# Rows of the last layer norm loaded into other buffers ahead of the accumulator rows, and three output tiles instead of two taking the bias by accumulating stores

## The chip, the cores and the metric

The kernel runs on one core of a Trainium2 chip. The metric is the device time of one execution in microseconds, here the median of three executions. One further execution was taken with the hardware profiler, and all rows below come from that one.

## What is computed

One layer of a post-norm decoder over 512 tokens of width 1024: a layer norm, a mixer with three branches, a residual layer norm, then a hierarchical mixture of experts and the last layer norm. The change lies in the last line of this part of the reference; `f` is the sum of the experts' outputs per token.

```python
x = layer_norm(ALPHA * x + m, ln1_g[l], ln1_b[l])
f = hierarchical_moe(x, w_rg[l], b_rg[l], w_re[l], b_re[l], w_up[l], w_down[l])
x = layer_norm(ALPHA * x + f, ln2_g[l], ln2_b[l])

def layer_norm(x, g, b):
    xf = x.astype(jnp.float32)
    mu = jnp.mean(xf, axis=-1, keepdims=True)
    var = jnp.mean(jnp.square(xf - mu), axis=-1, keepdims=True)
    y = (xf - mu) * lax.rsqrt(var + LN_EPS)
    return (y * g.astype(jnp.float32) + b.astype(jnp.float32)).astype(x.dtype)
```

## The kernel before

All arithmetic is fp32, with matrix products made of three passes over high and low parts. The experts' work is cut into 18 blocks of at most 128 tokens (`seq`, `nb` = 18), most of them one expert each. A block gathers its token rows, multiplies by the up weights, gates, and multiplies by the down weights (`down_mm`, L1211). The results of blocks 0 to 14 are copied from PSUM to a buffer named `yb` (`down_ev`, L1226; three buffers that take turns) and added to the rows of a DRAM accumulator `acc_d` by an indirect DMA of GpSimd with addition (`scatter`, L1232). The results of the last three blocks stay on chip (`down_split`, L1240) and are added by matrix products with 0/1 matrices `oht` that put each row at its token.

The end works on four tiles of 128 tokens. `acc_load(t)` (L1237) fetches tile t of the accumulator (512 KB) from DRAM by SyncE's queue. `combine(t, n)` (L1437) makes six matrix products for one half (512 columns) of a tile and adds them on VectorE to the accumulator row, with the row sum as a by-product. `ln2_var(t)` (L1447) makes the negative mean on VectorE and the sum of squares on ScalarE. `center(t)` (L1452) is two VectorE instructions, (x - mean) times `g2`. `rstd_ops` (L119) is a chain of tiny VectorE instructions for 1/sqrt(var): ten for several tiles at once, eight for one tile. `finish(t, r)` (L1456) scales by 1/sqrt(var) and stores: for tiles 0 and 1 ScalarE multiplies and GpSimd issues one store with addition onto `out`, which already holds the bias; for tiles 2 and 3 VectorE multiplies and adds `b2`, and SyncE issues plain stores of half a tile.

The bias was put into `out` long before, at L954 to L956, by one DMA of ScalarE's queue that repeats the row `ln2_b` over the first 256 rows. The rows `ln2_g` and `ln2_b` for the end, each repeated over 128 partitions (512 KB), are loaded at L1386 to L1395 into `raw3`, a buffer that held an expert's down weights before.

Order is fixed by hand (`manual_schedule`): each engine and each DMA queue runs its instructions in the order of the program, and waits on semaphores for the rest. A buffer that takes turns is written again only when its last user is done. On SyncE's queue the order is: the last weight loads (L750), the two norm rows (L1392), the four accumulator tiles (L1238), the four plain stores (L1463). `weave(chain, fill)` (L143) sets the instructions of `fill` evenly between those of `chain`. After the end stands a branch for extra blocks (L1485), which was not entered in the profiled execution; at its exit GpSimd's sequencer waits for its DMAs, and at the program's exit (L1582) all engines meet.

Of the kernel before, what the change touches and what calls it, by code (L numbers as in the profile page):

```python
# [9 lines left out]
F32 = mybir.dt.float32  # L10
# [7 lines left out]
P = 128  # L18
D = 1024
# [19 lines left out]
EPS2 = EPS / ALPHA ** 2  # L39
# [14 lines left out]
def trunk(ctx, tc, x, mem, rows, cols, wz, wkv, pac, pb8, pb2, wax, ws, wo, wr, br, we, out):  # L54
    nc = tc.nc
    pe, dve, act, pool, sp = nc.tensor, nc.vector, nc.scalar, nc.gpsimd, nc.sync
# [86 lines left out]
    def weave(chain, fill=()):  # L143
        done = 0
        for i, f in enumerate(chain):
            f()
            while done * len(chain) < (i + 1) * len(fill):
                fill[done]()
                done += 1
# [100 lines left out]
    with ExitStack() as st_a:  # L250
# [106 lines left out]
        rstd, ops = rstd_ops(mv)  # L357
# [561 lines left out]
    for i in range(2 * NT):  # L919
        j = i - 1  # L920
        ps = mmps()
        mm_pair(i, ps, 0)
        if i == 6:
            ohe = so2.tile([P, NT, P], F32, name="xr2")
        if i:
            r_tr(j)
        if 0 < i < 5:
            prep_hi(0, i - 1)
        mm_pair(i, ps, 1)
        if i:  # L930
            router(j)
        if i and i % 2 == 0:
            t = i // 2 - 1
            ln1_tile(t)
            weave(scale_ops(t, 512, (0, 512)))
            put_x1(sp, t)
        if 0 < i < 5:
            prep_lo(0, i - 1)
        if i == 5:
            ops, rest = route_ops(0, 2)  # L940
            weave(ops)
        mm_pair(i, ps, 2)
        if i == 5:
            rank_mm(0)
            rank_mm(1)
        if i == 6:
            weave(pos_ops(0, 2) + rest)
        if i == 7:
            ops, rest = route_ops(2, 3)
            weave(ops)  # L950
        mm_pair(i, ps, 3)
        for e, u in pending.get(i, ()):
            load_unit(e, u)
        if i == 1:  # L954
            r = ROWS.index("ln2_b")
            act.dma_start(out[:2 * P, :], rows[r:r + 1, :].to_broadcast([2 * P, D]))  # L956
        if i == 7:
            rank_mm(2)
        wo_add(i, ps)
        wo_stats(i)  # L960
        if i + 3 < 2 * NT:
            load_xr(i + 3)
    t = NT - 1
# [341 lines left out]
    for b in range(nb):  # L1305
        p_ = seq[b]
        nxt = seq[b + 1] if b + 1 < nb else p_
        pu = up_mm(b)
        if b == 0:
            sp.dma_start(seen_d, xgi[1][0:1, 0:4])  # L1310
            for e, u in ((2, 1), (3, 0), (3, 1), (4, 0), (4, 1)):
                load_unit(e, u)
            dn_hi(0, 0)
            dn_hi(0, 1)
            pw = map_mm(ohs_s, NS, 1, 3)
            gws = map_gw(pw, NS, "s")
            h = gate_h(pu, gws, NS - 1)
            hT = h_ev(h_tr(h))
            dn_lo(0, 0, dve, None)
            transp(1)  # L1320
            dn_lo(0, 1, dve, None)
            pdn[0] = down_mm(0, hT)
            scatter(down_ev(pdn[0]), *where(0)[::2])
        elif b > 1:
            hT = h_ev(pth)
        if b == 3:
            blk["ixx"] = map_ix(pix, NCOLX, "x")
            gather(5, *where(5)[::2])
            gather(6, *where(6)[::2])
            weave(vals_x)  # L1330
            pwx = map_mm(ohs_x, NCOLX, 1, 3)
        if b == 4:
            blk["gwx"] = map_gw(pwx, NCOLX, "x")
        ix, gw, c = where(b)
        new = [seq[b - 1]] if b and (b == 1 or seq[b - 2] != seq[b - 1]) else []
        if b == nb - 1:
            break

        def dn_prep():
            for p1 in new:  # L1340
                pl = pools[p_] if nxt != p_ else xp if pools[p_] is hlp else hlp
                for n in range(2):
                    if b > 1:
                        dn_hi(p1, n)
                        dn_lo(p1, n, dve, pl)
                if at[p1] + 3 < E:
                    load_unit(order[at[p1] + 3], 2)

        if b == nb - 2:
            scatter(down_ev(pdn[b - 2]), *where(b - 2)[::2])  # L1350
        dn_prep()
        tail = []
        if b == 1:
            load_unit(order[5], 0)
        if b and nxt != p_:
            for i in range(3):
                prep_hi(nxt, i)
        if 3 < b < nb - 2:
            yb = down_ev(pdn[b - 2])
        held = b > 1 and seq[b - 2] == seq[b - 1]  # L1360
        if b and nxt != p_:
            if not held:
                prep_hi(nxt, 3)
            if b == 1:
                ops = oe_b + order_tokens()
                weave(ops[:8], [lambda i=i, c=c_: prep_lo(nxt, i, None, c, c + 512) for i in range(2) for c_ in (0, 512)])
                weave(ops[8:18], [lambda c=c_: prep_lo(nxt, 2, None, c, c + 512) for c_ in (0, 512)])
                tail = ops[18:] + [lambda: prep_lo(nxt, 3)]
            else:
                ops = []  # L1370
                if b == 2:
                    ohs_x, ops, vals_x = map_ops(blk["px"], blk["ohx"], NCOLX, "x")
                weave(ops[:5] or [lambda: None] * 3, [lambda i=i: prep_lo(nxt, i) for i in range(3)])
                tail = ops[5:] if held else ops[5:] + [lambda: prep_lo(nxt, 3)]
        if b and nxt != p_:
            for i in (2 * at[p_] + 9, 2 * at[p_] + 10):
                if i < 2 * E:
                    load_unit(order[i // 2], i % 2)
        if b:
            h = gate_h(pu, gw, c)  # L1380
        if 0 < b < nb - 1:
            transp(b + 1)
        weave(tail)
        if b + 4 < nb and b not in (1, 2):
            gather(b + 4, *where(b + 4)[::2])
        if b == nb - 2:  # L1386
            gb2 = mlate.tile([P, 2048], F32, name="raw3")
            g2, b2 = gb2[:, :D], gb2[:, D:]

            def load_gb(eng, i):  # L1390
                r = ROWS.index("ln2_g") + i
                eng.dma_start((g2, b2)[i], rows[r:r + 1, :].to_broadcast([P, D]))  # L1392

            load_gb(sp, 0)
            load_gb(sp, 1)  # L1395
        if 3 < b < nb - 2:
            scatter(yb, *where(b - 2)[::2])
        if b == nb - 4:
            oht = mox.tile([P, 4, T], F32R, name="rawx", bufs=2)
            row_hot(oht[:, 0], *where(nb - 3)[::2])  # L1400
        if b == nb - 3:
            for i in range(1, 3):
                row_hot(oht[:, i], *where(nb - 3 + i)[::2])
        if b > 1:
            pdn[b - 1] = down_mm(b - 1, hT)
            if b == nb - 2:
                ys.append(down_split(pdn[b - 1]))
            elif b < 3:
                scatter(down_ev(pdn[b - 1]), *where(b - 1)[::2])
        if b:  # L1410
            pth = h_tr(h)
        if held:
            prep_half(nxt, 3)
        if b == 2:
            pix = map_mm(ohs_x, NCOLX, 0, 1)
# [21 lines left out]
    def combine(t, n):  # L1437
        ns = halves_[n]
        ps = (mmps if n and t else auxps)()
        for i in range(3):  # L1440
            for k in range(2):
                pe.matmul(ps, lhsT=oht[:, i, t * P:(t + 1) * P], rhs=ys[i][:, k, ns],  # L1442
                          start=i + k == 0, stop=i + k == 3)
        dve.scalar_tensor_tensor(xs_[t][:, ns], ps, 1.0, xs_[t][:, ns], op0=ALU.mult, op1=ALU.add,
                                 accum_out=sums[:, t, n:n + 1])
# [8 lines left out]
                                                       op0=ALU.add, op1=ALU.mult) for ns in halves_]  # L1454

    def finish(t, r):  # L1456
        if t < 2:
            act.mul(zs[t], zs[t], r)
            pool.dma_start(out[t * P:(t + 1) * P, :], zs[t], accum_op=ALU.add)
        else:  # L1460
            for ns in halves_:
                dve.scalar_tensor_tensor(zs[t][:, ns], zs[t][:, ns], r, b2[:, ns], op0=ALU.mult, op1=ALU.add)
                sp.dma_start(out[t * P:(t + 1) * P, ns], zs[t][:, ns])  # L1463
# [4 lines left out]
        combine(t, 1)  # L1468
        ln2_var(t)
    weave(center(0))  # L1470
    r01, ops = rstd_ops(None, 2, sums[:, 0:2, 3], EPS2)
    weave(ops, [lambda: combine(2, 0), lambda: combine(2, 1), lambda: ln2_var(2)] + center(1))
    finish(0, r01[:, 0:1])
    finish(1, r01[:, 1:2])
    combine(3, 0)
    combine(3, 1)
    ln2_var(3)
    weave(center(2) + center(3))
    r23, ops = rstd_ops(None, 2, sums[:, 2:4, 3], EPS2)
    weave(ops)  # L1480
    finish(2, r23[:, 0:1])
    finish(3, r23[:, 1:2])

    n_extra = nc.values_load(blk["eix"][0:1, NEXTRA:], min_val=0, max_val=E - 1)
    with tc.If(n_extra > 0):  # L1485
# [100 lines left out]
```

## Time and profile before

| | us |
|---|---|
| Median of three executions (lowest, highest) | 917.89 (917.84, 918.22) |
| The profiled execution, its own time | 920.99 |
| Its span, first to last instruction | 919.2 |
| TensorE busy in it | 883.4 (96%) |
| VectorE busy | 588.8 (64%) |
| ScalarE busy | 460.6 (50%) |
| GpSimd busy | 58.1 (6%) |

Moments are given in us from the start of the span. The profiled execution took 3.1 us longer than the median of the others. The busy share is a mean over the whole span; the change touches only the last 60 us of it and one store near 643 us.

### The profile page before, as it was taken

How to read it: one execution, taken by the hardware profiler on the slowest of the kernel's cores; microseconds unless marked ns; L12 is line 12 of the kernel's file. 1: busy time of each engine (PE TensorE's matmuls, PEld its weight loads, DVE VectorE, ACT ScalarE, POOL GpSimd, SP SyncE). 2: the span in 40 equal slices, each digit the busy share in tenths (PEclk: the TensorE clock that was granted, in tenths of full speed). 3: DMA queues.
4: the chain of work that ended last, by engine and by line, in shares of the span. 5: the costliest groups of instructions: out<-in, count | busy, mean ns of one | idle time of the engine just before them, and what ended most of it. 6: DMA issues, size and time to landing. Idle time of an engine off the chain costs nothing.

```text
span 919.2 us, 11177 instructions
## 1 busy us (share of the span) xinstructions
PE 883.4 (96%) x4272; PEld 733.8 (80%) x4272; DVE 588.8 (64%) x1020; ACT 460.6 (50%) x656; POOL 58.1 (6%) x59
## 2 busy tenths in 40 slices
PE   9999999999999999999999999999998889999991
PEld 5778888889998888888878888788887678888870
DVE  6765773344555543345866865766768887689976
ACT  5545432223444342214678687534204657688942
POOL 0000100000000000000000000000001123233210
PEclk9999999999999999999999999999997989999996
DMA  8313632333322412221313322237673988899544
GB/s 339 123 46 115 218 126 97 112 112 109 121 93 92 142 46 91 102 79 73 129 62 106 138 73 88 92 109 279 229 286 112 409 320 274 269 285 405 146 151 96
DMA packets 29281, 144.70 MB, mean 157 GB/s; under 512 B 5461, under 2 KB 5717, under 8 KB 16166
## 3 DMA queue, kind: packets, MB, share of 16 engines
q1 hardware_dynamic: 21462, 127.25, 37.6%
q0 software_dynamic: 6048, 13.45, 5.8%
q10 hardware_dynamic: 1712, 3.24, 1.1%
q8 instruction: 35, 0.57, 0.3%
q14 instruction: 24, 0.20, 0.1%
HBM read 136.24 MB, written 17.30 MB: 167 GB/s over the span
## 4 chain that ended last, share of the span: by engine, by line
PE 78%; DVE 11%; ACT 5%; DMA 3%; issue 2%; SPq 0%; DVEq 0%; ACTq 0%
PE mm L109 61%; PE mm L1220 4%; PE aux L109 4%; PE mm L308 3%; DVE hl L767 2%; PE aux L1162 1%; DMA x<-in_x_dram 1%; DMA col<-in_cols_dram 1%; ACT hl L82 1%; PE aux L1442 1%; DMA o<-in_we_dram 1%; DVE hl L83 1%; PE aux L464 1%; DVE xs L83 1%; ACT hl L1200 1%
## 5 line engine op out<-in xcount | busy, mean ns | idle before, releaser
L109 PE MATMUL mm<-hl 128*128 128x512 f32 x1416 | 327.6, 390 | 0.2 <-DVE hl L83 0.2
L109 PEld LDWEIGHTS mm<-hl 128*128 128x128 f32 x1416 | 264.7, 188 | 54.6 <-DVE hl L83 0.6
L83 DVE TENSOR_TENSOR hl<-raw,hl 128x1024 fp32r<-128x1024 f32 (+1 forms) x116 | 136.3, 1181 | 136.7 <-ACT hl L82 136.2
L82 ACT CAST hl<-raw 128x1024 fp32r<-128x1024 f32 (+1 forms) x116 | 116.3, 1015 | 126.3 <-PE mm L109 113.8
L109 PE MATMUL mm<-o,hl 128*128 128x512 f32 x624 | 142.9, 389 | 1.2 <-ACT o L82 1.2
L109 PEld LDWEIGHTS mm<-o,hl 128*128 128x128 f32 x624 | 117.1, 188 | 25.8 <-ACT o L82 1.6
L109 PE MATMUL mm<-hl,xs 128*128 128x512 f32 x408 | 99.7, 401 | 0.0
L109 PEld LDWEIGHTS mm<-hl,xs 128*128 128x128 f32 x408 | 77.1, 193 | 15.9
L767 DVE TENSOR_TENSOR hl<-o,hl 128x1024 fp32r<-128x1024 f32 (+1 forms) x45 | 50.3, 1147 | 4.8 <-ACT hl L761 4.7
L1220 PE MATMUL mm<-hl,hT 128*128 128x512 f32 x196 | 49.5, 399 | 0.0
L761 ACT CAST hl<-o 128x1024 fp32r<-128x1024 f32 x42 | 41.9, 1051 | 4.2 <-PE mm L1220 4.2
L1220 PEld LDWEIGHTS mm<-hl,hT 128*128 128x128 f32 x196 | 35.6, 188 | 6.8
L1086 POOL DMA_INDIRECT y<-x_d,ixg x3 | 3.2, 1070 | 594.5 <-DVE rtl L1145 593.9
L224 ACT ACTIVATE gate<-mm,col 128x512 f32<-128x512 f32 x24 | 16.5, 688 | 39.7 <-PE mm L109 39.6
L1209 DVE TENSOR_TENSOR hl<-raw,hl 128x1024 fp32r<-128x1024 f32 x26 | 30.6, 1220 | 3.2 <-PE mm L109 1.6
L1200 ACT CAST hl<-raw 128x1024 fp32r<-128x1024 f32 x32 | 31.9, 1053 | 0.0
L109 PE MATMUL mm<-memT,hl 128*128 128x256 f32 x192 | 27.3, 286 | 0.2 <-ACT memT L82 0.2
L308 PE MATMUL mm<-o,hl 128*128 128x512 f32 x96 | 25.8, 421 | 0.9 <-ACT hl L82 0.6
L109 PEld LDWEIGHTS mm<-memT,hl 128*128 128x128 f32 x192 | 24.9, 191 | 0.9 <-ACT memT L82 0.4
L808 ACT COPY x1T<-aux 128x512 f32<-128x512 f32 x8 | 4.7, 587 | 40.6 <-PE aux L807 25.9
L109 PE MATMUL mm<-hl,yh 128*128 128x512 f32 x96 | 24.4, 400 | 0.0
L109 PE MATMUL mm<-hl,memT 128*128 128x256 f32 x192 | 24.3, 283 | 0.0
(337 smaller groups left out, 1157.8 us busy)
## 6 DMA issues: line engine op xcount, KB each, us to landing
raw<-in_wz_dram SPq DMA_DIRECT2D x30, 1024.0 KB, 4.7
o<-in_we_dram SPq DMA_DIRECT2D x21, 1024.0 KB, 8.0
raw<-in_we_dram SPq DMA_DIRECT2D x18, 1024.0 KB, 7.5
rawx<-in_we_dram SPq DMA_DIRECT2D x9, 1024.0 KB, 7.8
raw<-in_pac_dram SPq DMA_DIRECT2D x8, 1024.0 KB, 4.7
raw<-in_wkv_dram SPq DMA_DIRECT2D x8, 1024.0 KB, 4.7
raw<-in_pb_dram SPq DMA_DIRECT2D x4, 1024.0 KB, 6.2
raw<-in_wo_dram SPq DMA_DIRECT2D x4, 1024.0 KB, 4.9
```

The source lines that it names most:

```text
L82: act.copy(hi, src)
L83: dve.tensor_tensor(lo, src, hi.bitcast(F32), op=ALU.subtract)
L109: pe.matmul(ps, lhsT=a(sa_), rhs=b(sb_), start=first and i == 0, stop=last and i == 2)
L224: act.activation(store[j], ps, AF.Sigmoid, bias=cc(C_M + br_i * 8 + j))
L308: pe.matmul(ps, lhsT=xT(k, slice(t * P, (t + 1) * P))(sx), rhs=wv[2 * n + k // 4, k // 2 % 2][:, sw, k % 2, :], start=i == 0, stop=i == 23)
L464: pe.matmul(pv[:, ch * P:(ch + 1) * P], lhsT=v[:, ch, g * P:(g + 1) * P], rhs=wst[:, g, :], start=True, stop=True)
L761: act.copy(t[:, 0], raws[key, i // 2][:, (i % 2) * 1024:(i % 2 + 1) * 1024])
L767: (eng or dve).tensor_tensor(t[:, 1, c0:c1], src[:, c0:c1], t[:, 0, c0:c1].bitcast(F32), op=ALU.subtract)
L1162: pe.transpose(ps[:, j * P:(j + 1) * P], xg[:, k * P:(k + 1) * P], ident)
L1200: act.copy(dnh[key][:, :, n * 512:(n + 1) * 512], dn_half(key, n))
L1209: eng.tensor_tensor(dnl[key][n], dn_half(key, n), dnh[key][:, :, ns].bitcast(F32), op=ALU.subtract)
L1220: pe.matmul(ps, lhsT=hT[:, sa_, f, :], rhs=dn[sb_][:, f, :], start=i + f == 0, stop=i + f == 3)
```

## The change

The diff in full. The initial bias store covers three tiles instead of two. The two norm rows go into two `yb` buffers instead of `raw3`; on SyncE's queue they keep their place ahead of the accumulator tiles. Tile 2 is finished as tiles 0 and 1 are. The chain for 1/sqrt(var) is made once for tiles 0 to 2 and once for tile 3 alone, and `center`, `combine` and `ln2_var` are ordered anew around it.

```diff
         if i == 1:
             r = ROWS.index("ln2_b")
-            act.dma_start(out[:2 * P, :], rows[r:r + 1, :].to_broadcast([2 * P, D]))
+            act.dma_start(out[:3 * P, :], rows[r:r + 1, :].to_broadcast([3 * P, D]))
...
         if b == nb - 2:
-            gb2 = mlate.tile([P, 2048], F32, name="raw3")
-            g2, b2 = gb2[:, :D], gb2[:, D:]
+            g2, b2 = (mo.tile([P, D], F32, name="yb", bufs=3) for _ in range(2))
...
     def finish(t, r):
-        if t < 2:
+        if t < 3:
             act.mul(zs[t], zs[t], r)
             pool.dma_start(out[t * P:(t + 1) * P, :], zs[t], accum_op=ALU.add)
         else:
...
         combine(t, 1)
         ln2_var(t)
     weave(center(0))
-    r01, ops = rstd_ops(None, 2, sums[:, 0:2, 3], EPS2)
-    weave(ops, [lambda: combine(2, 0), lambda: combine(2, 1), lambda: ln2_var(2)] + center(1))
-    finish(0, r01[:, 0:1])
-    finish(1, r01[:, 1:2])
-    combine(3, 0)
-    combine(3, 1)
+    combine(2, 0)
+    combine(2, 1)
+    ln2_var(2)
+    weave(center(1))
+    r012, ops = rstd_ops(None, 3, sums[:, 0:3, 3], EPS2)
+    weave(center(2))
+    weave(ops, [lambda: None, lambda: combine(3, 0), lambda: None, lambda: combine(3, 1)])
+    finish(0, r012[:, 0:1])
     ln2_var(3)
-    weave(center(2) + center(3))
-    r23, ops = rstd_ops(None, 2, sums[:, 2:4, 3], EPS2)
+    finish(1, r012[:, 1:2])
+    finish(2, r012[:, 2:3])
+    weave(center(3))
+    r3, ops = rstd_ops(None, 1, sums[:, 3:4, 3], EPS2)
     weave(ops)
-    finish(2, r23[:, 0:1])
-    finish(3, r23[:, 1:2])
+    finish(3, r3[:, 0:1])
```

## Rows read from the trace of the kernel before

**Rows 1.** Waits of 880 to 920 us: waiter, releaser, total us, times, longest.
```profile
DVE y L1444 <- DMA y<-acc_d: 3.8, 1, 3.8
```
**Rows 2.** SyncE queue's own waits, 800 to 920 us, same columns.
```profile
SPq L1392 <- DVE o L1209: 24.7, 1, 24.7
```
**Rows 3.** Timeline of the end: start us, us, engine, line, operation, operands, count.
```profile
886.42 0.81 SPq L1392 DMA_DIRECT2D raw<-in_rows_dram  x2
887.40 2.17 SPq L1238 DMA_DIRECT2D y<-acc_d  x4
888.33 4.24 PE L1442 MATMUL aux<-hl,rawx 128*128 128x512 f32 x18
889.15 0.69 DVE L83 TENSOR_TENSOR hl<-mm,hl 128x512 fp32r<-128x512 f32 x1 [0.67 <-ACT hl L82]
893.60 0.69 DVE L1444 SCALAR_TENSOR_TENSOR y<-aux,y 128x512 f32<-128x512 f32 x1 [3.76 <-DMA y<-acc_d]
895.13 1.52 PE L1442 MATMUL mm<-hl,rawx 128*128 128x512 f32 x6
896.54 1.41 DVE L1453 SCALAR_TENSOR_TENSOR o<-y,ln2s,raw 128x512 f32<-128x512 f32 x2
897.99 0.17 DVE L125 TENSOR_SCALAR lnv<-ln2s 128x2 f32<-128x2 f32 x1
901.83 0.15 DVE L135 SCALAR_TENSOR_TENSOR lnr<-lnt,lnr 128x2 f32<-128x2 f32 x1
902.02 2.19 ACT L1458 ACTIVATE o<-o,lnr 128x1024 f32<-128x1024 f32 x2 [0.64 <-DVE lnr L135]
903.46 1.91 POOL L1459 DMA_DIRECT2D out_dram<-o  x2 [26.71 <-DVE ln2s L1449]
904.11 1.13 ACT L1450 ACTIVATE yb<-y,ln2s 128x1024 f32<-128x1024 f32 x1
906.02 0.16 DVE L125 TENSOR_SCALAR lnv<-ln2s 128x2 f32<-128x2 f32 x1
907.99 2.74 DVE L1462 SCALAR_TENSOR_TENSOR o<-o,lnr,raw 128x512 f32<-128x512 f32 x4
908.76 2.51 SPq L1463 DMA_DIRECT2D out_dram<-o  x4
```
**Rows 4.** GpSimd's accumulating stores of the end, L1459: issue to landing.
```profile
DMA to landing us min/median/max: 5.8/7.5/9.2
```
**Rows 5.** Last scatters, L1233, 858 to 877 us: duration min/median/max ns, starts; landing.
```profile
L1233 POOL DMA_INDIRECT acc_d<-yb,ix_x x3: 1545/1597/4546, 858.5 to 872.2; - x3
...
DMA to landing us min/median/max: 6.1/6.2/8.9
```
**Rows 6.** GpSimd's sequencer at the exit, L1485, then L1582: ns, starts.
```profile
L1485 POOLq EVENT_SEMAPHORE  x1: 7858/7858/7858, 905.9 to 905.9; - x1
L1485 POOLq INC_SWDGE_SEM  x1: 1031/1031/1031, 913.8 to 913.8; - x1
...
L1582 POOLq DRAIN  x1: 3498/3498/3498, 914.9 to 914.9; - x1
```
**Rows 7.** SyncE's sequencer at the exit, L1582: ns, first and last start.
```profile
L1582 SPq DRAIN  x2: 7/10/13, 917.5 to 917.6; - x2
```
**Rows 8.** SyncE's plain stores of the end, L1463: issue to landing.
```profile
DMA to landing us min/median/max: 5.5/5.6/5.6
```
**Rows 9.** Accumulator loads, L1238: issue to landing.
```profile
DMA to landing us min/median/max: 6.1/7.3/8.1
```
**Rows 10.** DMA packets, 904 to 914 us: queue, packets, MB, share of 16 engines.
```profile
q0 software_dynamic: 288, 1.05, 67.9%
q1 hardware_dynamic: 492, 0.91, 23.9%
```
**Rows 11.** DMA packets, 906.5 to 908 us, same columns.
```profile
q0 software_dynamic: 72, 0.29, 101.1%
```
**Rows 12.** The bias store near 643 us, L956: issue to landing.
```profile
DMA to landing us min/median/max: 9.9/9.9/9.9
```

## The prediction

> **What bounds the kernel now.** TensorE is busy 96% of the span, but the change lies behind its last matrix product, so I read the end in this order: the waits, the timeline, the landings of the stores, and last what each engine does at the exit. The first view shows one wait worth having: VectorE stands still for 3.76 us until the first accumulator tile arrives [rows 1, 3]. The products for it began at 888.33 and run 18 in 4.24 us, so the first six end near 889.7; VectorE was free at 889.84, and it starts only at 893.60. Why the tile is late is seen in SyncE's own waits: the load of the norm rows waits 24.7 us, till the split of the last down weights frees `raw3` [rows 2]. It goes out at 886.42, and the accumulator tiles stand behind it at 887.40; the first lands 6.1 us later [rows 3, 9].
>
> From 893.60 VectorE has no gap worth the name until 910.73, when the last half tile is done; its plain store goes out at about 910.8 and lands 5.5 us later, at 916.3 [rows 3, 8]. That looks like the end, and the chain of waits also ends on VectorE and SyncE. But SyncE is through with its exit work at 917.6 [rows 7], while the span ends at 919.2. The one who is later is GpSimd's sequencer: it waits 7.86 us from 905.9 for its accumulating stores, which is until 913.76, then spends 1.03 us on a semaphore instruction and 3.50 us in a drain, to 918.4 [rows 6]. This fits the landing of the second accumulating store, issued at about 904.5 and landed 9.2 us later [rows 3, 4]. So the end is set by the last accumulating store plus 919.2 - 913.76 = 5.44 us, and SyncE's path has some 0.8 us to spare. What the change does to that store decides.
>
> **The change, part by part.** *Norm rows into `yb`.* The two `yb` buffers belonged to the scatters issued at 858.5 and 865.3, landed some 6.1 and 6.2 us later, about 864.6 and 871.5 [rows 5]. SyncE's queue then has nothing else, so the rows load there and leave the way free. `acc_load` next waits for the last scatter, 872.2 + 8.9 = 881.1. Issued then with 6.1 us to the first landing, tile 0 is there by 887.3, before its products at 889.7: the 3.76 us of waiting go. The row loads share DMA engines with the two last scatters, so these may land up to about 1.4 us later each (512 KB at 380 GB/s, an estimate from 0.91 MB in 23.9% of 10 us [rows 10]); even with 2.4 us more the tile is in time. The junk buffer moves to the last scatter's `yb`, free at 881.1 and first needed after 891: nothing.
>
> What is late next is TensorE: with the data there, VectorE follows the products, six per 1.4 us, and gains nothing until the sixth half tile, whose products end at 895.13 + 1.52 = 896.65 [rows 3]. Center of tile 0 and the rest fit between.
>
> *New order on VectorE.* From 896.7: combine 0.7, mean 0.2, centers of tiles 1 and 2 at 1.41 each [rows 3] give 900.4. The ten small steps then have a pitch of 0.2 us (906.02 to 907.99 is ten of them without fill [rows 3]) and two combines of about 0.65 between them: 3.0 to 3.3 us, so 1/sqrt(var) for tiles 0 to 2 is there at about 903.4. Before, tiles 0 and 1 had it at 901.98 [rows 3]. So although 3.76 us of waiting are gone, the first ScalarE multiply starts 1.4 us later than before, since a third tile's statistics and center now lie ahead of it. For VectorE as a whole the end comes sooner: the two instructions that finished tile 2 are gone (1.37), the second chain has eight steps for ten (0.4). Center of tile 3 from 903.6 to 905.0; its chain waits for ScalarE's squares (below, 905.8) and takes 1.6; two last instructions end at 908.9 instead of 910.73.
>
> *ScalarE.* In order: multiply 0, squares of tile 3, multiply 1, multiply 2. A multiply has a pitch of about 1.05 (2.19 for two), the squares 1.04 and a read of 0.19 behind [rows 3]. From 903.45 the multiplies end at 904.6, 906.8 and 907.9.
>
> *GpSimd.* Its store starts 0.29 us after the multiply's end (903.17 to 903.46) and occupies it about 0.94 [rows 3]. So three stores start at 904.9, 907.1 and 908.1, against two at 903.46 and 904.5.
>
> *The accumulating store of tile 2.* This is the dear part. Beside no plain store, 72 packets took 101.1% of all sixteen DMA engines for 1.5 us and moved 0.29 MB [rows 11]: 194 GB/s, so 512 KB is 2.70 us of all engines. Plain packets need 23.9% of 10 us for 0.91 MB [rows 10]: 0.69 us for 256 KB, half as much per byte. The whole of the two accumulating stores with their slow start was 6.79 us, plain work beside it 2.39: 9.2 us, which is the time from the first store's issue done (904.40) to the second's landing (913.7). After the change: 6.79 + 2.70 + two plain stores of 0.69 each, 1.38, all of which now fall into this stretch = 10.9 us, counted from 905.8. Last landing 916.8; with 5.44 behind it the span ends at 922.3, 3.1 us later. The unknown is how evenly the sixteen engines share: lower bound with no plain store in the way 915.4, span 920.9; upper bound with a late engine as the second store had it (9.2 against 2 x 2.70 + about 2 of start), 1.9 more, span 924.2.
>
> *Bias store of three tiles.* One DMA either way, 1.5 instead of 1.0 MB, landed 9.9 us after issue near 643 [rows 12]. Half as much again lands at most 5 us later, and nobody touches `out` before 903. The loads beside it are for steps further on (`load_xr(i + 3)`, L962, three half tiles ahead), and TensorE works on meanwhile. I take nothing; if that cover were gone, at most those 5 us.
>
> A rule of the Trainium skill, "DMA: Bandwidth & Descriptors" (section on the anatomy of one DMA on GpSimd's path), speaks against my price: a DMA there costs about 2.0 us plus its bytes at 436 GB/s. For 512 KB that would be an estimated 3.2 us, so the third store would land near 911.3 and the span would end near 916.7. The trace does not agree: these stores took 5.8 and 9.2 us [rows 4], and while they had the engines to themselves they moved 194 GB/s [rows 11].
>
> **The rivals.** *The third store costs no time of its own.* If the stores overlap freely, the last lands as the first did alone, 5.8 us after its start: 908.1 + 5.8 = 913.9, where the last one lands now. The span is 919.3 and the time 918.0, no change. Faster still, down to the rate of plain packets: then SyncE's plain stores decide. The last goes out at 908.9, lands at 914.4, and 1.3 + 0.8 us of exit make 916.5, a time of 915.2. It decides from an accumulating landing before 911.1. The rule above of the Trainium skill, "DMA: Bandwidth & Descriptors", would lead close to this case. For it: early in the stretch the engines move little. Against it: a full DMA share right after.
>
> *The drain is no fixed cost behind the last store.* The 3.50 us of drain could wait for something else, which will be over. Then the end is 916.8 + 1.03 + 0.1 + 0.8 = 918.7, a time of 917.4, no change. For it: the drains of SyncE take 10 ns [rows 7]. Against it: GpSimd's begins right behind its own semaphore instruction, and nothing else in the rows ends at 918.4.
>
> *The change doesn't bring the accumulator tiles early* (the last scatter later than 885, or SyncE held up). Then VectorE starts near 893.6 as now, center of tile 0 ends at 897.95, and the chain is there at about 905.4 instead of 903.4: 2.0 us on top, a time of 923.0. The gaps that TensorE's pace would leave take up the rest.
>
> **How the numbers follow.** The profiled execution's span is 919.2 and its own time 920.99, 3.1 above the median 917.89; I take differences of the span and set them on the median. Forecast: 917.89 + 3.1 = 921.0, chance 0.62, own range 919.7 to 922.9. Third store for nothing: 0.07 no change, 0.11 faster. Drain not fixed: 0.15, no change. Tiles not early: 0.05. A measurement of this kernel tells some 0.2% (1.8 us) from no change. Slower 0.67, same 0.22, faster 0.11. The range 917.3 to 923.3 takes in forecast, the drain, the late tiles and the free store without gain; what is left out is the faster case and the ends.
>
> **What would show it.** Right: the wait of 3.8 us on `y<-acc_d` is gone, norm rows go out near 865 and 872, accumulator tiles near 881 to 883; first multiply of ScalarE near 903.4; stores of GpSimd near 904.9, 907.1, 908.1; its long semaphore wait ends near 917, about 5.4 us ahead of the end, and SyncE is ready some 5 us before. Wrong: a last accumulating landing before 914 (its price per byte was mistaken), or an end less than 3 us behind it (the drain was).

## The result, and the profile after

The changed kernel takes 923.91 us (median of four executions, 923.11 to 924.94) against 918.06 in the same session, a ratio of 1.0058 (95% interval 1.0045 to 1.0070); a second measurement of both on another occasion gave 924.22 and 1.0066 (1.0052 to 1.0079). It is slower, as forecast, and by more: the forecast was 921.0, 3.1 us above the kernel before, with 923.3 as upper end; the medians of the session differ by 5.85 us.

The waits of the end, 880 to 920 us, and SyncE's own from 800 us (waiter, releaser, total us, times, longest) answer to [rows 1, 2]:

```profile
DVE y L1443 <- DMA y<-acc_d: 1.8, 1, 1.8
...
SPq L1391 <- DMA acc_d<-yb,ix_x: 19.0, 2, 10.8
...
SPq L1238 <- DMA acc_d<-yb,ix_x: 6.4, 1, 6.4
```

VectorE's wait for the first accumulator tile has fallen from 3.8 to 1.8 us. SyncE no longer waits for a split of weights; it waits for the scatters. The timeline of the end, with the lines that answer to [rows 3] (line numbers are one lower there and in some kernels below):

```profile
886.70 1.75 SPq L1238 DMA_DIRECT2D y<-acc_d  x4
886.72 4.24 PE L1441 MATMUL aux<-hl,rawx 128*128 128x512 f32 x18
890.07 0.69 DVE L1443 SCALAR_TENSOR_TENSOR y<-aux,y 128x512 f32<-128x512 f32 x1 [1.84 <-DMA y<-acc_d]
901.61 1.15 ACT L1457 ACTIVATE o<-o,lnr 128x1024 f32<-128x1024 f32 x1 [4.19 <-DVE lnr L135]
903.06 0.94 POOL L1458 DMA_DIRECT2D out_dram<-o  x1 [20.90 <-ACT o L1457]
903.80 2.17 ACT L1457 ACTIVATE o<-o,lnr 128x1024 f32<-128x1024 f32 x2
905.23 0.87 POOL L1458 DMA_DIRECT2D out_dram<-o  x1 [1.23 <-DVE lnt L129]
905.59 1.41 DVE L1461 SCALAR_TENSOR_TENSOR o<-o,lnr,yb 128x512 f32<-128x512 f32 x2
906.26 0.84 POOL L1458 DMA_DIRECT2D out_dram<-o  x1 [0.17 <-issue]
906.37 1.00 SPq L1462 DMA_DIRECT2D out_dram<-o  x2
```

VectorE is done at 907.0 and the last plain store is out at 907.4, yet the span ends at 921.4. What lies between is the landing of GpSimd's stores and GpSimd's exit (landing after issue in us; then its sequencer's lines, duration in ns and start, as in [rows 4, 6]; then SyncE's as in [rows 7]):

```profile
DMA to landing us min/median/max: 5.7/6.8/9.2
...
L1487 POOLq EVENT_SEMAPHORE  x2: 43/4031/8019, 907.4 to 915.8; - x2
L1487 POOLq INC_SWDGE_SEM  x1: 1042/1042/1042, 915.9 to 915.9; - x1
...
L1584 POOLq DRAIN  x1: 3580/3580/3580, 917.0 to 917.0; - x1
...
L1584 SPq DRAIN  x2: 7/10/13, 917.7 to 917.7; - x2
```

The third store, issued at 906.26, lands 9.2 us later, near 915.4; GpSimd waits for it from 907.4 for 8.02 us, then spends 1.04 and 3.58 us, to 920.6. SyncE has been ready since 917.7, 3.7 us ahead of the end instead of the some 5 that were forecast.

The start of an execution moves by one to two us from one to the next whatever the kernel, so the kernels are compared below from the first product of the first combine (the line of TensorE at 886.72 above) to the end of the span, "the end" for short: 921.4 - 886.7 = 34.7 us here, 919.2 - 888.3 = 30.9 in the kernel before [rows 3].

### The profile page after: what moved, and what is told of

It reads as the page before. It is cut to its first block, busy times and chain, and to the rows that moved or that the text cites. A ratio compares the mean times of both kernels' runs of the same rounds, so it can differ in the third digit from the quotient of the medians.

```text
span 921.4 us, 11177 instructions
## 1 busy us (share of the span) xinstructions
PE 883.0 (96%) x4272; PEld 732.8 (80%) x4272; DVE 587.4 (64%) x1016; ACT 462.4 (50%) x657; POOL 68.0 (7%) x60
## 4 chain that ended last, share of the span: by engine, by line
PE 77%; DVE 12%; ACT 5%; DMA 2%; issue 2%; SPq 0%; ACTq 0%; POOLq 0%; POOL 0%; DVEq 0%
PE mm L109 61%; PE mm L1220 4%; PE aux L109 4%; PE mm L308 3%; DVE hl L767 2%; PE aux L1162 1%; DMA x<-in_x_dram 1%; DMA col<-in_cols_dram 1%; ACT hl L82 1%; DVE hl L83 1%; PE aux L464 1%; ACT hl L1200 1%; ACT hl L761 1%; DVE th L684 0%; PE aux L564 0%
## 5 line engine op out<-in xcount | busy, mean ns | idle before, releaser
L1220 PEld LDWEIGHTS mm<-hl,hT 128*128 128x128 f32 x196 | 36.4, 193 | 6.9
L1200 ACT CAST hl<-raw 128x1024 fp32r<-128x1024 f32 x32 | 31.9, 1053 | 0.0
L1233 POOL DMA_INDIRECT acc_d<-yb,ix_x x10 | 27.0, 2703 | 54.3 <-ACT hl L761 20.5
```

What stands on the lines that cost most here:

```text
L1200: act.copy(dnh[key][:, :, n * 512:(n + 1) * 512], dn_half(key, n))
L1220: pe.matmul(ps, lhsT=hT[:, sa_, f, :], rhs=dn[sb_][:, f, :], start=i + f == 0, stop=i + f == 3)
L1233: pool.indirect_dma_start(out=acc_d[:, :], in_=yb, in_offset=None, out_offset=bass.IndirectOffsetOnAxis(ap=ix[:, b:b + 1], axis=0), bounds ...
```

## The experiments

Nine kernels beside the two were run, and the two themselves again. Two of the nine leave something out: the one with plain GpSimd stores the bias of tiles 0 to 2, the one without the third store the result of tile 2. The table gives the measured ratio to the kernel before of the same session, and three distances from the first combining product, read from each profile: the issue of the first accumulating store, GpSimd's semaphore instruction that follows the last landing, and the end of the span.

| Kernel | Ratio (95%) | First store | Semaphore | End |
|---|---|---|---|---|
| before, on record | 1 | 15.1 | 25.5 | 30.9 |
| before, second profile | 1.0004 (0.9993, 1.0014) | 14.9 | 24.0 | 29.4 |
| before, third profile | 1.0004 (0.9994, 1.0014) | 15.3 | 24.6 | 30.0 |
| bias store of three tiles only | 0.9997 (0.9987, 1.0008) | 14.8 | 25.4 | 30.8 |
| norm rows moved only | 0.9984 (0.9975, 0.9993) | 13.4 | 22.8 | 28.2 |
| changed, early chain | 1.0021 (1.0012, 1.0030) | 13.4 | 25.8 | 31.3 |
| changed, tile 2 plain | 1.0036 (1.0023, 1.0049) | 16.3 | 26.4 | 32.3 |
| changed, no third store | 1.0031 (1.0019, 1.0043) | 16.3 | 26.0 | 31.9 |
| changed, plain GpSimd stores | 1.0015 (1.0005, 1.0025) | 16.3 | 25.0 | 30.5 |
| changed | 1.0058 (1.0045, 1.0070) | 16.3 | 29.2 | 34.7 |
| changed, again | 1.0066 (1.0052, 1.0079) | 16.3 | 29.6 | 35.0 |
| changed, rows late | 1.0083 (1.0070, 1.0096) | 18.2 | 30.9 | 36.4 |
| rows moved, all tiles plain | 0.9996 (0.9986, 1.0005) | none | none | 28.8 |
| rows moved, one accumulating store | 0.9975 (0.9965, 0.9986) | 13.4 | 20.0 | 27.7 |

**The kernel before, again.** No edit.

> The kernel before, unchanged, for a second profile of it. The one on record ran 3.1 us above the median, so the difference of the two profiles (2.2 us) falls short of the difference of the medians (5.9). Theory 1 (the end decides: the last accumulating landing plus a fixed exit): from the first product of the first combine to the end of the span it is 30.9 us again (888.3 to 919.2), and a span near 916.3 means that the stretch before it was some 3 us shorter in this execution. Theory 2 (the body differs between the kernels): the end is the same, but the stretches before it are steady and shorter than the changed kernel's.

Its profile has a span of 916.1 and starts the combining products at 886.71; the end is 29.4 us, not 30.9. GpSimd's semaphore instruction of this execution:

```profile
L1485 POOLq INC_SWDGE_SEM  x1: 1031/1031/1031, 910.7 to 910.7; - x1
```

So neither theory holds whole. 1.6 us of the difference between the two profiles of this kernel lie ahead of the end (888.33 against 886.71), and 1.5 us lie in the end itself. A body that differs between the kernels is not seen: the combining products start at 886.71 here and at 886.72 in the changed kernel. Of the 1.5 us, 1.3 lie in the landing of the second accumulating store: from its first store's issue to that semaphore instruction it is 910.7 - 901.6 = 9.1 us, on record 913.8 - 903.5 = 10.3 [rows 3, 6].

**Only the norm rows moved.**

```diff
-            gb2 = mlate.tile([P, 2048], F32, name="raw3")
-            g2, b2 = gb2[:, :D], gb2[:, D:]
+            g2, b2 = (mo.tile([P, D], F32, name="yb", bufs=3) for _ in range(2))
```

> The kernel before with only the two norm rows moved to the yb buffers. Theory 1: VectorE starts 2 to 3.5 us earlier after the first product, held by TensorE's pace afterwards, so the two accumulating stores are issued about 2.3 us earlier and land as much earlier: 915.7, faster by 2.3 us (1.5 to 3.0). Theory 2 (row loads in the stretch of the last scatters slow the body): no gain or a loss, 918 to 920.

917.09 us, a ratio of 0.9984: 1.5 us faster, at the lower end of theory 1. The first store is issued 13.4 us after the first combining product instead of 14.9 to 15.3. The rows' move is a gain. The last scatter is issued at 881.0 here and at 870.1 to 872.2 in the three profiles of the kernel before, but with the rows late it also comes at 881.4 and 882.2 (larger bias store, rows late again), and with the rows early at 872.9 and 873.4 (one accumulating store, early chain). So the rows' move alone does not decide it.

**Tile 2 stored plainly.** The changed kernel with

```diff
-            act.dma_start(out[:3 * P, :], rows[r:r + 1, :].to_broadcast([3 * P, D]))
+            act.dma_start(out[:2 * P, :], rows[r:r + 1, :].to_broadcast([2 * P, D]))
-        if t < 3:
+        if t < 2:
```

> The changed kernel with tile 2 finished on VectorE and stored plainly, and the bias put into two tiles only; order and row loads as changed. Theory 1: the third accumulating store (2.7 us of all DMA engines) is gone, two plain half-tile stores take its place, and the last accumulating landing comes 2 us sooner: 1.5 to 3 us below the changed kernel, still 1 to 3 us above the kernel before, since the first two stores start late. Theory 2 (the larger bias store near 643 us costs in the body): the whole 5.9 us go, the time is that of the kernel before.

1.0036: 2.0 us below the changed kernel, 3.3 above the kernel before. With two accumulating stores as before and the rows early, it is still slower than the kernel before, so the third store isn't the whole loss; the new order is left.

**The rows late again.** The edit of the second experiment taken back out of the changed kernel.

> The changed kernel with the norm rows in raw3 again. Theory 1: VectorE starts with the late accumulator tiles, the chain for 1/sqrt(var) is 1.5 to 2.5 us later and the end with it: 1.5 to 2.5 us above the changed kernel. Theory 2 (row loads in the stretch of the last scatters cost more than they bring): the changed kernel's time or below it.

1.0083, 2.3 us (0.0025 of 918) above the changed kernel's first ratio and 1.6 above its second; the first store 18.2 us after the first product instead of 16.3. Theory 1.

**GpSimd's stores without addition.** The changed kernel with

```diff
-            pool.dma_start(out[t * P:(t + 1) * P, :], zs[t], accum_op=ALU.add)
+            pool.dma_start(out[t * P:(t + 1) * P, :], zs[t])
```

> The changed kernel with GpSimd's three stores made plain, without addition; this leaves out the bias of tiles 0 to 2. Same issue times, same bytes. Theory 1 (the addition makes a store twice as dear on the DMA engines, 2.7 us for 1.4): the three stores take some 4 us of engine time for 9.5, the third lands about 5 us after its issue, near 911 to 912 on the changed profile's clock instead of 915.4: 3 to 4 us below the changed kernel. Rival (a GpSimd store has its price from being issued in software, or from HBM at the end): within 1 us of the changed kernel.

1.0015, 3.9 us below the changed kernel (4.7 by its second ratio), with the stores issued at the same distances from the first product. DMA packets (queue, packets, MB, share of 16 engines) of this kernel from 905 to 914 us, its stores' landing, and the changed kernel's packets from 904 to 916 us:

```profile
q0 software_dynamic: 432, 1.57, 44.2%
...
DMA to landing us min/median/max: 3.5/4.2/5.0
```

```profile
q0 software_dynamic: 432, 1.57, 74.0%
q1 hardware_dynamic: 288, 0.52, 12.9%
```

The same 1.57 MB take 44.2% of 9 us plainly, 1.3 us a store, and 74.0% of 12 us with addition, 3.0 us a store. The edit takes out nothing but the addition, so it is the addition that makes a store dear, not GpSimd's queue.

**All tiles plain.** The kernel with only the rows moved, and

```diff
-            act.dma_start(out[:2 * P, :], rows[r:r + 1, :].to_broadcast([2 * P, D]))
+            pass
-        if t < 2:
+        if t < 0:
```

> The kernel with only the row loads moved, and all four tiles finished on VectorE with plain stores of SyncE; no bias store, no accumulating store. Theory 1 (GpSimd's 1.0 us and 3.5 us of exit hang on the last accumulating landing alone): GpSimd is through its exit long before SyncE, the end is the last plain landing plus about 2.1 us; VectorE has four instructions of 0.69 more, so 1 to 2.5 us above the kernel with only the rows moved, near the kernel before. Rival (the drain stands behind the last work of whatever kind): the drain of 3.5 us follows the plain landings, 4 to 6 us above the kernel with only the rows moved.

0.9996, 1.1 us above the kernel with only the rows moved, though the two intervals overlap. GpSimd's exit here follows the last scatter (its semaphore instruction, its drain), and SyncE's drain alone stands before the end at 916.9:

```profile
L1484 POOLq INC_SWDGE_SEM  x1: 987/987/987, 887.9 to 887.9; - x1
...
L1581 POOLq DRAIN  x1: 3335/3335/3335, 888.9 to 888.9; - x1
...
L1581 SPq DRAIN  x2: 7/10/13, 915.6 to 915.7; - x2
...
DMA to landing us min/median/max: 3.1/3.1/3.1
```

The drain takes 3.3 us in the middle of the products, 23 us before the last plain store is issued. So it belongs to GpSimd's exit and waits for nothing of the end. The last row is the landing of the plain stores: 3.1 us here; in the three profiles of the kernel before, where accumulating stores were under way, the median was 5.6 [rows 8], 4.3 and 5.0.

**No third store.** The changed kernel with `if t < 2:` ahead of GpSimd's store.

> The changed kernel without the third accumulating store and nothing in its place; this leaves out tile 2's result, its rows hold the bias alone. Theory 1 (the stores share the engines one after another): the last landing is that of the second store, 2.7 us or more sooner: 2.5 to 4 us below the changed kernel. Rival (the third store overlaps with the other two, the loss is all in the later first store): less than 1 us below.

1.0031, 2.5 us below the changed kernel (3.2 by its second ratio); the semaphore instruction comes 3.2 us sooner after the first product (26.0 against 29.2). Of these, 1.0 is the last store's earlier issue (18.5 against 19.5 after the first product) and 0.4 a gap between landing and semaphore instruction that stands in the changed kernel; some 1.8 are left for the third store's own turn. It does not overlap freely.

**Only the larger bias store.** The kernel before with the first line of the change's diff.

> The kernel before with only the bias store near 643 us widened from 256 to 384 rows (the rows of tile 2 are written over at the end by the plain stores). Theory 1: no change, within 0.7 us of the kernel before. Rival (its 0.5 MB more delay loads in the body): 1 to 3 us above.

0.9997: nothing. Its end is that of the kernel before, and its profile shows a late second landing once more, 25.4 us after the first product, as on record; from the first store's issue to the semaphore instruction it is 10.6 us.

**The changed kernel, again.** No edit.

> The changed kernel, unchanged, for its time beside the kernel before on one chip and a second profile. Theory 1 (the end of the changed kernel was forecast rightly, from its first combining product to the last accumulating landing 28.5 us and 5.4 of exit, and the size was missed because the end of the kernel before was read from an execution whose second store landed late): from the first combining product to the end again 34 to 35.5 us, the last accumulating landing 28 to 29.5 after that product; 4.5 to 6 us above the kernel before. Rival (the first measurement of 5.9 us was a chance of few runs): 2.5 to 4 us above.

1.0066, 6.1 us, so the first measurement was no chance. Its end is 922.1 - 887.1 = 35.0 us:

```profile
887.09 4.24 PE L1441 MATMUL aux<-hl,rawx 128*128 128x512 f32 x18
903.44 0.94 POOL L1458 DMA_DIRECT2D out_dram<-o  x1 [20.90 <-ACT o L1457]
...
L1487 POOLq INC_SWDGE_SEM  x1: 1042/1042/1042, 916.7 to 916.7; - x1
```

**The early chain.** The changed kernel with 1/sqrt(var) of tiles 0 and 1 made as early as in the kernel before:

```diff
     weave(center(0))
-    combine(2, 0)
-    combine(2, 1)
-    ln2_var(2)
-    weave(center(1))
-    r012, ops = rstd_ops(None, 3, sums[:, 0:3, 3], EPS2)
+    r01, ops = rstd_ops(None, 2, sums[:, 0:2, 3], EPS2)
+    weave(ops, [lambda: combine(2, 0), lambda: combine(2, 1), lambda: ln2_var(2)] + center(1))
+    finish(0, r01[:, 0:1])
+    finish(1, r01[:, 1:2])
+    combine(3, 0)
+    r2, ops = rstd_ops(None, 1, sums[:, 2:3, 3], EPS2)
     weave(center(2))
-    weave(ops, [lambda: None, lambda: combine(3, 0), lambda: None, lambda: combine(3, 1)])
-    finish(0, r012[:, 0:1])
+    weave(ops, [lambda: None, lambda: combine(3, 1)])
+    finish(2, r2[:, 0:1])
     ln2_var(3)
-    finish(1, r012[:, 1:2])
-    finish(2, r012[:, 2:3])
     weave(center(3))
```

> The changed kernel with the chain for 1/sqrt(var) of tiles 0 and 1 early again, as in the kernel before, and one chain each for tiles 2 and 3; three accumulating stores and early row loads as changed. Theory 1 (the later first store costs as much as the third store itself): the first two stores go out as in the kernel with only the rows moved, 13.4 and 14.5 us after the first combining product, the third store follows their data without a gap and costs 2.5 to 3.5 us over the kernel with only the rows moved: 919.5 to 920.5, some 3 to 4.5 us below the changed kernel. Rival (the third store costs nearly all): within 1.5 us of the changed kernel.

1.0021: about 3.4 us below the changed kernel's first ratio, 4.1 below its second, and 3.4 above the kernel with only the rows moved. GpSimd's stores of this kernel, whose first product is at 887.76, and SyncE's accumulator loads:

```profile
901.18 1.91 POOL L1458 DMA_DIRECT2D out_dram<-o  x2 [24.99 <-ACT o L1457]
905.13 0.84 POOL L1458 DMA_DIRECT2D out_dram<-o  x1 [2.05 <-ACT o L1457]
...
880.71 1.75 SPq L1238 DMA_DIRECT2D y<-acc_d  x4
```

Three stores, the first 2.9 us sooner after the first product than in the changed kernel (13.4 against 16.3), and the end is 3.4 to 3.8 us shorter (31.3 against 34.7 and 35.0). So the loss has two halves, the late first store and the third store. Set out from the kernel before, by the ratios: the rows' move gives 1.5 us, the third store costs 3.4, the one chain for three tiles another 3.4 to 4.1.

**The kernel before, a third profile.** No edit.

> The kernel before, unchanged, for a further profile, to see how far the landing of its second accumulating store moves between executions. Theory 1: from the start of its first store's issue to the second's landing it is 9 to 10.5 us, the execution on record (10.3) at the upper end; the rest of the end is the same within 0.3 us.

From the first store's issue to the semaphore instruction 9.4 us (903.71 to 913.1). The three profiles give 10.3, 9.1 and 9.4; the one on record is the longest. With the 10.6 of the larger bias store, whose end is the same, such a length is not rare.

**One accumulating store.** The kernel with only the rows moved, and

```diff
-            act.dma_start(out[:2 * P, :], rows[r:r + 1, :].to_broadcast([2 * P, D]))
+            act.dma_start(out[:P, :], rows[r:r + 1, :].to_broadcast([P, D]))
-        if t < 2:
+        if t < 1:
```

> The kernel with only the row loads moved, with tile 0 alone taking the bias by an accumulating store and tiles 1 to 3 stored plainly. Theory 1 (GpSimd's exit hangs on the last accumulating landing, SyncE's on the last plain one, and plain stores land sooner where no accumulating store shares the engines): one accumulating store lands 6 us after its issue, GpSimd is through 25 us after the first combining product; VectorE takes 1.4 us more, the last plain store goes out 22.1 after that product and lands some 3 to 4 us later instead of 5, end at 27.2 to 28.3: 0 to 1 us below the kernel with only the rows moved, 1.5 to 2.5 below the kernel before. Rival (VectorE's extra 1.4 us decide): 1 to 1.5 us above the kernel with only the rows moved.

916.46 us, a ratio of 0.9975: 2.3 us faster than the kernel before and the fastest of all that were run, though its interval (0.9965 to 0.9986) overlaps that of the kernel with only the rows moved. The one store lands after 6.6 us and the plain ones after 3.0:

```profile
DMA to landing us min/median/max: 6.6/6.6/6.6
...
DMA to landing us min/median/max: 2.0/3.0/3.1
```

GpSimd is through its exit at 911.5, and the end at 914.7 follows the last plain landing. So a third accumulating store was the wrong way; whether one is better than two is not shown, and none at all (0.9996) is not better.

## Why the prediction was right in its direction and short in its size

**What sets the end: right.** GpSimd's exit behind the last accumulating landing decided, 5.4 us from the semaphore instruction to the end in all profiles of the kernel before. That the drain is a fixed cost was open; the kernel with all tiles plain shows it, and the rival that rested on the other reading falls.

**The wait for the accumulator: half right, and of no weight.** The tiles were forecast to go out at 881.1; they went out at 886.70, because the last scatter landed later, and 1.84 us of the wait were left. In the early-chain kernel they did go out at 880.71, VectorE began 1.6 us after the first product, and the first store was still issued 13.4 us after it, as in the kernel with only the rows moved, where VectorE began after 3.5. TensorE's pace covers that much, as the forecast said of the first half tiles.

**The new order: right.** The first multiply on ScalarE was forecast 15.1 us after the first product and came at 14.9; the three stores at 16.6, 18.8 and 19.8, and came at 16.3, 18.5 and 19.5. The condition of the rival of the late tiles came about (the last scatter landed after 885), but its price did not: VectorE began 3.4 us after the first product instead of 5.3, and the first multiply was on time. The kernel with late rows gives that price, 1.6 to 2.3 us (forecast: 2.0).

**The third store: right in kind.** The three stores were forecast at 6.79 + 2.70 = 9.5 us of engine time and took 8.9 (74.0% of 12 us), so the price in engine time was not too small. The rival that the third costs nothing falls: leaving it out gave 2.5 to 3.2 us. The rule of the Trainium skill, "DMA: Bandwidth & Descriptors" (its section on the anatomy of a DMA on GpSimd's path), would make it an estimated 3.2 us from issue to landing: the plain stores agree roughly (3.5 to 5.0), the accumulating ones do not (5.7 to 9.2). The last landing was forecast 28.5 us after the first product and came at 28.7, and at 29.1 in the second profile, where GpSimd's long wait ends at 916.2.

**The sum: the step that failed.** Means of the two profiles of the changed kernel less means of the three of the kernel before, in us:

| Part of the end | Forecast | Measured |
|---|---|---|
| First product to the first store's issue | +1.4 | +1.2 |
| End of that issue to the last landing | +1.7 | +3.0 |
| Last landing to the end | 0 | +0.5 |
| Sum, before rounding | +3.1 | +4.8 |

The step that failed is the second part: the stretch up to the last landing was set equal to the engine time of all packets, 9.2 us before and 10.9 after. In the changed kernel the engine time was 10.4 us in both profiles, below the forecast, and yet the stretch took 11.5 and 11.8. The packets (queue, packets, MB, share of 16 engines) of the changed kernel in this stretch, 904.0 to 915.46 us; in its last 0.96 us; and in the last 1.26 us of the same stretch of the kernel before, 912.5 to 913.76:

```profile
q0 software_dynamic: 432, 1.57, 77.5%
q1 hardware_dynamic: 288, 0.52, 13.5%
```

```profile
q1 hardware_dynamic: 17, 0.02, 5.5%
q0 software_dynamic: 8, 0.01, 4.6%
```

```profile
q1 hardware_dynamic: 241, 0.44, 90.9%
q0 software_dynamic: 6, 0.02, 6.7%
```

In both kernels the accumulating queue has next to nothing left to move for the last microsecond before the landing. In the kernel before, four plain stores fill that microsecond, and the sum counted their packets as if the landing waited for them. In the changed kernel the two plain stores have 17 packets left by then, so the engines stand almost empty and engine time no longer adds up to the stretch. The other profiles agree: in the last microsecond before the landing the plain queue took 99.6 and 95.8% and the accumulating one 2.2 and 6.6% in the two others of the kernel before, 1.3 and 2.1% in the second of the changed kernel. That the sum met 9.2 us in the kernel before was luck in part. Of the 1.3 us that are missing in this row, about 0.7 are the changed kernel's longer stretch (11.6 on average for 10.9).

The other 0.6 are the base (8.6 on average for 9.2). The stretch took 9.4 us in the execution on record, 8.1 and 8.4 in the two others of the kernel before; the longest was subtracted as if it were typical. The warning stood in the table: that execution was 3.1 us above the median of the others.

The last row was put at nothing: the semaphore instruction came 0.4 to 0.5 us behind the last landing, where the kernel before had it at once, and the drain took 3.58 us instead of 3.50, so the exit was 5.9 instead of 5.44. One more semaphore instruction of GpSimd's sequencer stands in that gap; that it is the reason is not shown.

The span itself, forecast at 922.3, came close (921.4 and 922.1), by luck: the first product came 1.6 and 1.2 us sooner than in the execution on record, and the end was 0.7 and 1.1 longer than forecast.

What stays open: the ratios say 5.3 and 6.1 us, the ends 4.8. The profiled executions of the kernel before lay on average 1.1 us above the medians of their sessions, those of the changed kernel 0.6 below. Ahead of the first combining product these profiles show the changed kernel 0.9 us shorter, not longer. So where the rest lies is not shown. The larger bias store, put at nothing, is not it (0.9997), though it landed 12.8 us after its issue instead of 9.9.

## What to carry to other kernels

When the last thing to finish is a transfer, cost the engine that waits for it to its very end: here the queue that looked last (SyncE) had 0.8 us to spare, and the end hung on GpSimd's stores, their addition and 5 us of exit. Work moved from a busy engine to an idle queue is paid where that queue ends; and an order that makes one chain serve three tiles holds back the first tile's store for the third tile's statistics. Engine time adds up to a landing only as far as the engines are full until then; look at the last microsecond of the stretch by itself. Before subtracting a span, look whether the profiled execution is a typical one: take a second profile, and compare stretches from a common event.

## What the runs showed of the hardware

With three queued, an accumulating store of 512 KB took 3.0 us of all sixteen DMA engines and a plain one from the same queue 1.3. Beside accumulating stores the plain ones of SyncE landed after 5.6, 4.3 and 5.0 us (medians of the three profiles of the kernel before) and after 5.8 and 6.9 in the changed kernel, without them after 3.1.

For the last microsecond before the last accumulating landing the accumulating queue took no more than 6.7% of the sixteen engines in all five profiles of the two kernels.

GpSimd's exit took 1.0 us for the semaphore instruction and 3.3 to 3.6 us for the drain in every profile, also in the middle of the products.

Issuing one of the last scatters occupied GpSimd for 1.5 to 2.8 us in some cases and for 4.5 to 6.9 in others. In the changed kernel and, below it, the kernel before (timelines of GpSimd and VectorE):

```profile
858.56 5.91 POOL L1233 DMA_INDIRECT acc_d<-yb,ix_x  x1 [5.21 <-ACT hl L761]
859.55 3.49 DVE L767 TENSOR_TENSOR hl<-o,hl 128x1024 fp32r<-128x1024 f32 x3
862.96 0.47 DVE L1177 SCALAR_TENSOR_TENSOR h<-h,gw_x,mm 128x256 f32<-128x256 f32 x1
```

```profile
872.20 4.55 POOL L1233 DMA_INDIRECT acc_d<-yb,ix_x  x1 [5.35 <-ACT hl L761]
874.11 1.22 DVE L767 TENSOR_TENSOR hl<-rawx,hl 128x1024 fp32r<-128x1024 f32 x1
875.24 0.48 DVE L1177 SCALAR_TENSOR_TENSOR h<-h,gw_x,mm 128x256 f32<-128x256 f32 x1
```

Both ended 1.5 us after VectorE went from a row of instructions with two operands in SBUF to one that also reads PSUM (864.47 and 876.75), and so did the changed kernel's next one (issued at 869.03, done at 875.13, VectorE's change at 873.63). One more in the changed kernel, issued at 880.4 beside such a row, took only 1.7, so the pattern isn't without exception, and no experiment was made on it. The Trainium skill, "SBUF — State Buffer" (section on the two sides of SBUF), tells of a port pair that VectorE and GpSimd share: GpSimd cannot write descriptors while VectorE runs an instruction in a mode that takes both ports, and a VectorE instruction with two inputs in SBUF holds up only a GpSimd instruction that reads SBUF. Whether either is at work here, no run shows; the one issued at 880.4 speaks against it. The next scatter waits for the landing, so such a scatter moves the accumulator tiles; here TensorE's pace hid it.
